# A second pair of weight blocks per layer computed by Strassen's scheme, its weight sums added by VectorE

## The chip, the cores and the metric

The kernel runs on 1 core of one Trainium2 chip. Its metric is the device time of one execution in microseconds (us); before the change the median of 3 runs is 895.15 us (894.86 to 895.54). Five engines with instruction streams of their own work beside each other: PE (TensorE: matmuls; PEld, its weight loads), DVE (VectorE), ACT (ScalarE), POOL (GpSimd) and SP (SyncE, which mostly issues DMA transfers). They wait for each other through semaphores only, and each takes its own instructions in the order in which they are written.

## The reference

A decoder trunk of DEPTH = 2 layers on 256 tokens of width 2048, all in float32. Each layer normalises its input, projects it by one matrix w_in of 2048 x 7,444 into the parts of four groups of attention heads (fox, diff, moba, gla), multiplies each group's output by a gate, and maps the 2048 mixed columns back by w_out, 2048 x 2048:

```python
def hybrid_layer(x, layer_idx, norm_g, w_in, ...):
    h = rms_norm(x, norm_g)
    p = split_columns(jnp.einsum("bsd,de->bse", h, w_in))
    ...
    fox = forgetting_attention(...); fox = from_heads(fox) * jax.nn.silu(p["fox_g"])
    diff = differential_attention(...); diff = from_heads(rms_norm(diff, ...)) * jax.nn.silu(p["diff_g"])
    moba = moba_attention(...); moba = from_heads(moba) * jax.nn.silu(p["moba_g"])
    gla = gla_chunked(...); gla = from_heads(rms_norm(gla, ...)) * jax.nn.silu(p["gla_g"])
    mixed = jnp.concatenate([fox, diff, moba, gla], axis=-1)
    return x + jnp.einsum("bse,ed->bsd", mixed, w_out)
```

## The kernel before

**Three products per multiplication.** TensorE runs in a fast float32 format (fp32r) that keeps fewer bits. So each operand is split into hi, its rounding (`hi_of`, an ACT copy into fp32r), and lo, the residue (`lo_of`, a DVE subtraction), and a product is hi x hi + lo x hi + hi x lo. The normalised input lies transposed in `hTp` (hi and lo), the mixed rows in `mTh` and `mTl`.

**Steps.** The weights stream in from HBM in *steps*, in an order that `_steps` fixes. A plain step is two blocks of 128 rows of one block of up to 512 columns: 512 KB into one of 5 buffers `raw` (issued by SP), a rounding by ACT, a residue by DVE, and 2 x 2 x 3 = 12 matmuls into two PSUM banks (`mm`), one for each half of the tokens. Eight plain steps make a block. hi and lo have 4 buffers each (PART_BUFS), so the splitting runs at most three steps ahead of the multiplying.

**A pair by Strassen's scheme.** Two blocks of 512 columns (`NAMES`) form a 2 x 2 block product: the 256 tokens and the 2048 rows are halved too, and seven products ("forms" p1 to p7) take the place of eight. A form is four steps c0 to c3 of 6 matmuls each, all into one PSUM bank which the pair holds. p1, p2 and p4 multiply plain halves of hTp; p3, p5, p6 and p7 multiply sums of halves, which `sum_forms` computes once per layer and keeps in mTh and mTl. On the weights' side the sums grow in the four chunks of `xs` (called y in the code; the residual rows rest elsewhere meanwhile): y starts as the weights' block 12, then 11, 22 and 21 are added to it while p5, p6, p7 and p4 use it as it then stands. Before, GpSimd adds them by accumulating DMA transfers (`add_to_y`, line 1683). After its last step a form is taken from PSUM into the tile `left` or `right` (`pair_result`, line 1779), scaled by the row's norm: the first of a sum by ACT, the others by DVE with an addition. Matmuls of a later form wait until the bank has been read.

**Order.** The program is written by a planner that keeps a clock for every engine (`Times`, `emit`, `choose`): attention work waits in tasks and is put between the splitting wherever the planner sees an engine free. `MIDDLE` sets the order of the blocks, and `FORMS_AT` the places of the form steps: before, one pair per layer (moba_v and diff_v), at plain steps 3, 6 and 8 of ten blocks, so that a form step stands after every two or three plain ones. The output projection begins with the products of gla and fox, then diff, then moba; the attention results are turned by DVE transposes and two DMA transfers (`turned`) and split into mTh and mTl (`split_group`).

Of the kernel before, what the change touches and what calls it, by code (L numbers as in the profile page):

```python
# [45 lines left out]
BY_DMA = True  # L46
# [3 lines left out]
KEPT = 2  # L50
PATIENCE = 0
HORIZON = 1.5
URGENT_HI = 3.0
URGENT_LO = 2.5
STALL = 0.3
SAFE = 1.0
HANDOVER = 0.2
SOON = 0.5
WAITED = 0.5
EARLY = 4  # L60
LOADED = 6.0
WRITE = 5.0
READ = 7.5
ADDED = 9.5
ISSUE = 0.6
CONSTANT = 12.0
# [90 lines left out]
def _pair_steps(l, n):  # L157
# [3 lines left out]
    if not BY_DMA:  # L161
        raws.update({"p6": ("22",), "p4": ("21",)})
# [4 lines left out]
def _steps():  # L167
# [71 lines left out]
class Times:  # L239


    def __init__(self):
        self.now, self.last, self.ends, self.by, self.free = 0.0, 0.0, {}, {}, {}

# [3 lines left out]
    def of(self, *operands, kind=None):  # L248
        names = [self.name(a) for a in operands if hasattr(a, "shape")]
        return max((self.ends.get(z, 0.0) + HANDOVER * (self.by.get(z) != kind) for z in names), default=0.0)  # L250
# [16 lines left out]
class Timed:  # L267
# [20 lines left out]
    def move(self, out, src, us, **kw):  # L288
        return self.give(Op("d" + self.kind, partial(self.eng.dma_start, out, src, **kw), [src], [out], us))
# [81 lines left out]
def hybrid_trunk(  # L371
# [68 lines left out]
    def emit(op, task=None):  # L440
# [8 lines left out]
        elif op.kind[0] == "d":  # L449
            end = at + op.us  # L450
            if op.kind == "da":
                a_.tail = max(a_.tail, times.now) + ISSUE
        else:
# [5 lines left out]
            e.tail = max(at, e.tail) + us  # L459
            end = e.tail  # L460
# [98 lines left out]
    s4.younger = lambda: len({t.rank for t in tasks if t.rank < cur["task"].rank}) if cur["task"] else 0  # L559
# [113 lines left out]
    def constants():  # L673

        yield from until(("h", 0, 3))
        a_.move(ct, const, 4.5)
        w3 = s2.get([P, DEPTH, 256])
# [24 lines left out]
        a_.move(fb.rearrange("p l h -> p (l h)"), bcast_rows(fox_fb, 0, DEPTH * H), CONSTANT)  # L702
# [9 lines left out]
        for l in range(DEPTH):  # L712
            li = 0.8 - 0.6 * math.exp(-0.3 * l)
            v_.scalar_tensor_tensor(lam[:, l:l + 1], ls2[:, l, 0:1], li, ls2[:, l, 1:2], op0=OP.add, op1=OP.subtract)
            v_.tensor_scalar(dng[:, l:l + 1], dng[:, l:l + 1], 1.0 - li, None, op0=OP.mult)

# [1271 lines left out]
```

## Time and profile before

| | us |
|---|---|
| median of 3 runs | 895.15 (894.86 to 895.54) |
| profiled execution: span from first to last instruction | 891.2 |
| PE, PEld busy | 881.5, 750.8 |
| DVE, ACT, POOL busy | 662.2, 559.1, 60.0 |
| HBM traffic | 254 GB/s over the span |

The profile comes from one execution. Its time outside the span isn't listed; the median stands 3.95 us above its span. Busy times are of one engine each, so they overlap. A matmul's length is modelled and overlaps the next one's, so distances are read from starts.

### The profile page before, as it was taken

Reading aid. Unit: us, or ns where it says so; the run is one execution under the profiler, and the core shown is the slowest. Engines: PE = TensorE matmul, PEld = TensorE weight load, DVE = VectorE, ACT = ScalarE, POOL = GpSimd, SP = SyncE. Lnnn points to the kernel's source line nnn. Section 1 sums busy time; section 2 is a strip of 40 time slices with the busy share of each in tenths; the row PEclk is TensorE's granted clock in tenths of the full one; section 3 lists DMA queues with packets and bytes.
Section 4 is the critical chain, followed back from the end, with each engine's and each line's share of the span. In section 5 each row is a group of like instructions: output and inputs, shape, how many; then the busy total and the mean of one; then the engine's idle time right before and its main releaser. Section 6 shows DMA issues by size and latency. Waiting matters only on the chain.

```text
span 891.2 us, 12456 instructions
## 1 busy us (share of the span) xinstructions
PE 881.5 (99%) x4380; PEld 750.8 (84%) x4380; DVE 662.2 (74%) x943; ACT 559.1 (63%) x846; POOL 60.0 (7%) x87
## 2 busy tenths in 40 slices
PE   9999999999999999999999999999999999999996
PEld 7988889888887888888899888898888888888886
DVE  6689878878867967656679778879676788585583
ACT  7577675577646667644756876578644575693461
POOL 1010110000110000000000100110000100101000
PEclk9999999999999999999999999999999999999999
DMA  8889897747988685977798898878958978499742
GB/s 289 294 263 303 266 301 241 254 147 263 288 240 274 203 317 178 362 265 228 235 302 265 285 320 224 253 227 277 337 147 262 301 220 271 168 301 363 236 143 96
DMA packets 84142, 227.45 MB, mean 255 GB/s; under 512 B 9979, under 2 KB 30443, under 8 KB 83950
## 3 DMA queue, kind: packets, MB, share of 16 engines
q1 hardware_dynamic: 73336, 192.00, 63.9%
q0 software_dynamic: 9152, 33.03, 14.5%
q10 hardware_dynamic: 1590, 1.62, 0.5%
q8 instruction: 34, 0.56, 0.3%
q14 instruction: 30, 0.25, 0.1%
HBM read 204.06 MB, written 22.55 MB: 254 GB/s over the span
## 4 chain that ended last, share of the span: by engine, by line
PE 93%; DVE 2%; DMA 2%; issue 1%; ACT 1%; SPq 0%; POOLq 0%; POOL 0%; DVEq 0%; ACTq 0%
PE mm L466 79%; PE side L466 14%; DMA raw<-in_weights 2%; DVE lo L466 1%; DVE four L466 1%; ACT hi L466 1%; DMA far<-four 0%; DVE mTl L466 0%; ACT four L466 0%; ACT L466 0%; DVE raw L466 0%; DVE eight L466 0%; SPq L466 0%; POOLq L1984 0%; POOL rf L466 0%
## 5 line engine op out<-in xcount | busy, mean ns | idle before, releaser
L466 ACT ACTIVATE hi<-raw 128x1024 fp32r<-128x1024 f32 (+2 forms) x319 | 316.6, 1011 | 190.9 <-PE mm L466 110.2
L466 PE MATMUL mm<-hi,hTp 128*128 128x512 f32 (+1 forms) x1760 | 432.7, 381 | 1.2 <-ACT hTp L466 0.9
L466 DVE TENSOR_TENSOR lo<-raw,hi 128x1024 fp32r<-128x1024 f32 (+2 forms) x319 | 363.7, 1157 | 93.3 <-ACT hi L466 89.0
L466 PEld LDWEIGHTS mm<-hi,hTp 128*128 128x128 f32 x1760 | 321.5, 188 | 60.3 <-ACT hi L466 1.3
L466 PE MATMUL mm<-lo,hTp 128*128 128x512 f32 (+1 forms) x880 | 237.4, 380 | 0.1
L466 PEld LDWEIGHTS mm<-lo,hTp 128*128 128x128 f32 x880 | 162.4, 188 | 30.6 <-DVE lo L466 0.8
L466 PE MATMUL mm<-hi,mTh 128*128 128x512 f32 (+1 forms) x256 | 69.3, 377 | 0.0
L466 PE MATMUL mm<-lo,mTh 128*128 128x512 f32 (+1 forms) x256 | 69.0, 376 | 0.1
L466 PE MATMUL mm<-hi,mTl 128*128 128x512 f32 (+1 forms) x256 | 69.0, 376 | 0.0
L466 PEld LDWEIGHTS mm<-lo,mTh 128*128 128x128 f32 x256 | 46.2, 188 | 9.2 <-DVE lo L466 0.5
L466 PEld LDWEIGHTS mm<-hi,mTl 128*128 128x128 f32 x256 | 46.3, 188 | 8.8
L466 PEld LDWEIGHTS mm<-hi,mTh 128*128 128x128 f32 x256 | 46.0, 188 | 8.6 <-ACT hi L466 0.4
L466 ACT ACTIVATE four<-mm,rstd 128x512 f32<-128x512 f32 (+2 forms) x56 | 36.7, 667 | 26.3 <-PE mm L466 26.3
L466 POOL DMA_DIRECT2D four<-far x40 | 21.8, 546 | 444.0 <-DMA far<-four 193.5
L466 DVE STREAM_TRANSPOSE four<-four 128x1024 f32<-128x1024 f32 (+1 forms) x34 | 39.1, 1149 | 6.7 <-ACT four L466 6.3
L466 ACT ACTIVATE four<-four 128x512 fp32r<-128x512 f32 (+3 forms) x44 | 35.5, 819 | 12.6 <-DMA four<-far 8.8
L466 PEld LDWEIGHTS side<-four,four 128*128 128x128 f32 (+1 forms) x336 | 37.7, 190 | 3.9 <-issue 1.8
L466 PE MATMUL side<-four,four 128*128 128x128 f32 (+3 forms) x336 | 39.3, 281 | 0.0
L1686 POOL DMA_DIRECT2D xs<-in_weights x24 | 21.2, 900 | 169.5 <-DVE lo L466 36.2
L466 DVE TENSOR_TENSOR lo<-xs,hi 128x1024 fp32r<-128x1024 f32 x24 | 29.1, 1214 | 1.8 <-ACT hi L466 1.8
L466 ACT ACTIVATE mTh<-four 128x1024 fp32r<-128x1024 f32 x16 | 16.9, 1057 | 21.2 <-DVE four L466 21.1
L466 ACT ACTIVATE hi<-xs 128x1024 fp32r<-128x1024 f32 x24 | 25.4, 1060 | 7.1 <-PE mm L466 6.2
(146 smaller groups left out, 685.1 us busy)
## 6 DMA issues: line engine op xcount, KB each, us to landing
raw<-in_weights SPq DMA_DIRECT2D x271, 512.0 KB, 4.9
four<-far POOLq DMA_DIRECT2D x34, 512.0 KB, 6.7
far<-four SPq DMA_DIRECT2D x128, 128.0 KB, 3.9
raw<-in_weights SPq DMA_DIRECT2D x46, 348.0 KB, 5.1
xs<-in_weights POOLq DMA_DIRECT2D x24, 512.0 KB, 8.5
xs<-in_weights SPq DMA_DIRECT2D x8, 512.0 KB, 8.3
xs<-in_x SPq DMA_DIRECT2D x4, 512.0 KB
kept<-xs SPq DMA_DIRECT2D x1, 2048.0 KB, 10.6
```

Source lines behind the costliest of these rows:

```text
L466: op.do()
L1686: g_.eng.dma_start(ys[:, c], weights[at:at + P * 1024].rearrange("(p j c) -> p j c", p=P, j=2), accum_op=OP.add)
```

## The change

The pair diff_q and diff_k is computed by forms too, ahead of moba_v and diff_v, in both layers. The forms come in the order 1 5 3 6 7 2 4. The weights' sums are added by VectorE (`add_raw`): block 11, 22 and 21 arrive as `raw` for the forms p1, p3 and p2 anyway, and are added to y from there, after which the raw buffer is free; the accumulating transfers are gone. `pair_result` takes p1 out twice by ACT and everything else by DVE. The form steps stand where a table of 56 places per layer puts them, counted in plain steps of the layer, most of them closer together than before. The order of the blocks, the places where the residual rows come back (`X_AT`), and the planner's prices and rules change too. In layer 1 `sum_forms` reads the unsplit tiles of the input, which are kept until then, where it added hi and lo before.

```diff
-X_AT = (1, 5, 9, 13)
-MIDDLE = ("gla_v", "fox_q", "fox_k", "fox_v", "fox_g", "diff_q", "diff_k", "moba_q", "moba_k", "diff_g", "moba_g", "moba_v", "diff_v")
-NAMES = (("moba_v", "diff_v"),)
+X_AT = (5, 8, 11, 13)
+MIDDLE = ('gla_v', 'fox_k', 'fox_q', 'fox_v', 'fox_g', 'moba_q', 'diff_k', 'moba_k', 'moba_g', 'moba_v', 'diff_q', 'diff_g', 'diff_v')
+NAMES = (('diff_q', 'diff_k'), ('moba_v', 'diff_v'))
...
-FORMS_AT = {3: (3, 6, 8), 4: (3, 6, 8), 5: (3, 6, 8), 6: (3, 6, 8), 7: (3, 6, 8), 8: (3, 6, 8), 9: (3, 6, 8), 10: (3, 6, 8), 11: (3, 6, 8), 12: (3,)}
-FORM_ORDER = ("p2", "p5", "p3", "p1", "p6", "p7", "p4")
+FORMS_AT = ((33, 34, 34, 35, 36, 39, 39, 39, 41, 42, 43, 43, 43, 45, 47, 47,
...
+FORM_ORDER = ("p1", "p5", "p3", "p6", "p7", "p2", "p4")
+ADDED_BY_V = ("p1", "p3", "p2")
+LATE = FORM_ORDER[0] == "p1"
+STARTS = ("p1", "p5", "p6", "p2", "p4") if LATE else ("p1", "p5", "p2")
...
     for l in range(DEPTH):
         rest = deque(z for n in range(len(NAMES)) for z in _pair_steps(l, n))
-        for i, places in FORMS_AT.items():
-            own = [k for k, s in enumerate(steps) if s.get("block") == l * LAYER + i]
-            for z, at in enumerate(places):
-                steps.insert(own[0] + at + z, rest.popleft())
+        own = min(k for k, s in enumerate(steps) if s.get("block", -1) // LAYER == l)
+        for z, at in enumerate(FORMS_AT[l]):
+            steps.insert(own + at + z, rest.popleft())
...
+    def add_raw(s):
+        y = ys[:, s["c"]]
+        v_.tensor_add(y, y, s["raws"][0])
+        yield
+        y_at[s["c"]] = s["slots"][0][0] = times.of(y)
...
+        whole = [env["t", l, c] for c in range(4)] if l else None
...
+            if whole:
+                if len(terms) == 3:
+                    sums(v_.tensor_sub, terms[0], terms[2])
+                else:
+                    sums(v_.tensor_add if terms[0] > 0 else v_.tensor_sub, None, terms[1])
...
+        if f in ADDED_BY_V:
             y_at[c] = math.inf
-            added.append((end, partial(add_to_y, s, q)))
+            begin(add_raw(s), -1, 3)
...
+        if LATE:
+            if f == "p1":
+                evac(left[:, 0], 0)
+                evac(left[:, 1], 1)
+            elif f == "p5":
+                add(right[:, 1], 1, left[:, 1], OP.subtract)
+            elif f == "p3":
+                add(right[:, 0], 0, left[:, 0], OP.subtract)
+            elif f == "p6":
+                add(right[:, 0], 0, by=nr)
+            elif f == "p7":
+                add(right[:, 1], 1, by=nr)
+                add(left[:, 1], 1)
+                given(l, s["id"][1], 1, right)
+            elif f == "p2":
+                add(left[:, 0], 0)
+            else:
+                add(left[:, 1], 1)
+                given(l, s["id"][1], 0, left)
```

(`evac` is an ACT copy out of PSUM, `add` a DVE scalar_tensor_tensor on it.)

How instructions move is shown at three places. Numbers behind names tell one tile of a name from the next; "waits" names the engines whose semaphores a row waits for.

TensorE in layer 0, before, at the change from form p5 to form p3: the second of the two plain steps between them (hi_1291, lo_1292), then p3's first step in the pair's bank mm2 (hi_1311, lo_1312):

```order
L466 MATMUL mm1_1149<-hi_1291,hTp_112 128x512 [waits Activation_49]
L466 MATMUL mm1_1149<-hi_1291,hTp_112 128x512 x3
L466 MATMUL mm1_1149<-lo_1292,hTp_112 128x512 [waits DVE_49]
L466 MATMUL mm1_1149<-lo_1292,hTp_112 128x512
L466 MATMUL mm3_1150<-hi_1291,hTp_112 128x512 x4
L466 MATMUL mm3_1150<-lo_1292,hTp_112 128x512 x2
L466 MATMUL mm2_758<-hi_1311,mTh_113 128x512 [waits Activation_49]
L466 MATMUL mm2_758<-hi_1311,mTh_113 128x512
L466 MATMUL mm2_758<-hi_1311,mTl_114 128x512 x2
L466 MATMUL mm2_758<-lo_1312,mTh_113 128x512 [waits DVE_49]
L466 MATMUL mm2_758<-lo_1312,mTh_113 128x512
```

TensorE in layer 0 of the first pair, after, from form p3's last step (mm0, hi_1285 and lo_1286) to p6's first (hi_1295 and lo_1296):

```order
L478 MATMUL mm0_923<-hi_1285,mTh_113 128x512 [waits Activation_49]
L478 MATMUL mm0_923<-hi_1285,mTh_113 128x512
L478 MATMUL mm0_923<-hi_1285,mTl_114 128x512 x2
L478 MATMUL mm0_923<-lo_1286,mTh_113 128x512 [waits DVE_49]
L478 MATMUL mm0_923<-lo_1286,mTh_113 128x512
L478 MATMUL mm0_923<-hi_1295,mTh_113 128x512 [waits DVE_49,Activation_49]
L478 MATMUL mm0_923<-hi_1295,mTh_113 128x512
L478 MATMUL mm0_923<-hi_1295,mTl_114 128x512 x2
L478 MATMUL mm0_923<-lo_1296,mTh_113 128x512 x2
L478 MATMUL mm1_1213<-hi_1337,hTp_112 128x512 [waits Activation_49]
```

No plain step stands between these two forms, and p6's first matmul into mm0 waits for DVE, which has to take p3 out of mm0; before, p3's first matmul waited for nothing but its rounding by ACT.

VectorE in layer 0, before, at the same change from p5 to p3 (lo_1312 is p3's first residue; tq and eight belong to gla's attention):

```order
L466 TENSOR_TENSOR lo_1292<-raw_1171,hi_1291 128x1024 [waits DVE_49,DMAHW7_49,PE_49,Activation_49]
L466 TENSOR_TENSOR tq_97<-eight0_1184,four2_1096 64x2x64 x2
L466 TENSOR_TENSOR lo_1312<-raw_1245,hi_1311 128x1024 [waits DMAHW0_49,PE_49,Activation_49]
L466 TENSOR_TENSOR tq_97<-eight0_1184,four2_1096 64x2x64 x2
L466 TENSOR_TENSOR lo_1337<-raw_1268,hi_1336 128x696 [waits DMAHW1_49,PE_49,Activation_49]
L466 TENSOR_TENSOR tq_97<-eight0_1184,four2_1096 64x2x64 x3
L466 TENSOR_TENSOR eight0_1184<-eight0_1184,four2_1096 128x2x64
L466 TENSOR_TENSOR lo_1351<-raw_1281,hi_1350 128x696 [waits DMAHW2_49,PE_49,Activation_49]
```

VectorE in layer 0, after, at the change from p3 to p6 of the first pair (the rows xs<-xs,raw add weights, the last row takes p3 out of PSUM):

```order
L478 TENSOR_TENSOR lo_1262<-raw_1197,hi_1261 128x1024 [waits DMAHW1_49,PE_49,Activation_49]
L478 TENSOR_TENSOR xs_83<-xs_83,raw_1197 128x1024
L478 TENSOR_TENSOR qx_94<-eight0_911,four13_807 64x128 x2
L478 TENSOR_TENSOR lo_1286<-raw_1221,hi_1285 128x1024 [waits DMAHW2_49,PE_49,Activation_49]
L478 TENSOR_TENSOR xs_83<-xs_83,raw_1221 128x1024
L478 TENSOR_TENSOR lo_1296<-xs_83,hi_1295 128x1024 [waits PE_49,Activation_49]
L478 COPY_PREDICATED four2_910<-masks_84,side1_1301 128x8x16 [waits PE_49,Activation_49]
L478 COPY_PREDICATED four2_910<-masks_84,side1_1301 128x16x8 [waits DVE_49]
L478 COPY_PREDICATED four2_910<-masks_84,side1_1301 128x32x4 [waits DVE_49]
L478 TENSOR_TENSOR lo_1338<-raw_1248,hi_1337 128x1024 [waits DMAHW7_49]
L478 SCALAR_TENSOR_TENSOR four4_1189<-mm0_923,rstd_585,four0_1019 128x512 [waits PE_49]
```

Where one residue per step stood with attention's small operations between, a form step now has a residue and an addition, and the evacuation stands behind the residue of the step after next.

GpSimd, before, from the row norms of layer 0 on (xs<-in_weights are the accumulating transfers, four<-far are returns of turned rows):

```order
L466 TENSOR_TENSOR rstd<-pw,halfpow 128x2
L1686 DMA xs<-in_weights 128x1024 x5
L466 DMA four_1019<-far_1039 128x1024
L1686 DMA xs<-in_weights 128x1024 x2
L466 DMA four_1141<-far_1128 128x1024
L466 DMA four_1142<-far_1147 128x1024
L1686 DMA xs<-in_weights 128x1024
```

GpSimd, after, from the same place:

```order
L478 TENSOR_TENSOR rstd<-pw,halfpow 128x2
L478 DMA four_680<-far_723 128x1024
L478 DMA four_1101<-far_1099 128x1024
L478 DMA four_1226<-far_1228 128x1024
L478 DMA four_1553<-far_1605 128x1024
L478 DMA four_1831<-far_1841 128x1024
```

The 24 accumulating transfers are gone from GpSimd's queue; the returns of turned rows follow each other.

More of the change, by code (lines that the diff above doesn't have):

```diff
@@ L49 @@
 T4 = 14
-KEPT = 2
+KEPT = 1
 PATIENCE = 0
 HORIZON = 1.5
-URGENT_HI = 3.0
+URGENT_HI = 3.5
 URGENT_LO = 2.5
 STALL = 0.3
-SAFE = 1.0
+DELAY = 0.2
+LEAD = 3.0
+OVERLAP = 0.085
+SAFE = 1.5
 HANDOVER = 0.2
-SOON = 0.5
-WAITED = 0.5
-EARLY = 4
+SOON = 1.0
+WAITED = 0.8
+EARLY = 5
 LOADED = 6.0
-WRITE = 5.0
-READ = 7.5
-ADDED = 9.5
+WRITE = 4.0
+READ = 11
+ADDED = 12.5
 ISSUE = 0.6
+RATE = 340000.0
+LANDING = 3.2
 CONSTANT = 12.0
@@ L449, in emit @@
         elif op.kind[0] == "d":
-            end = at + op.us
+            end = times.land(at, op.moved, op.us)
             if op.kind == "da":
@@ L1182, in fox_forget @@
         yield
+        yield from until("loaded")
         v_.tensor_add(fx, fx, fb[:, l, None, :].to_broadcast([P, 2, H]))
@@ L1284, in diff @@
         yield from until(("diff_k", l))
+        yield from until("lam")
         yield
@@ L1526, in load_more @@
             s = plan[i]
-            if kind == "raw" and loads["out"] == RAW_BUFS and not (loads["freed"] and loads["freed"][0] <= by):
-                return
+            if len(loads["ring"]) == RAW_BUFS:
+                freed = loads["ring"][0][0]
+                if freed is None or freed > by:
+                    return
+                loads["ring"].popleft()
+            s.setdefault("slots", []).append([None])
+            loads["ring"].append(s["slots"][-1])
             if "pair" in s:
@@ L1532, in load_more @@
                 load(i)
-            if kind == "raw" and loads["out"] == RAW_BUFS:
-                loads["freed"].popleft()
-            else:
-                loads["out"] += kind == "raw"
             loads["next"] += 1
@@ L1635, in sum_forms, with sums @@
         z = yield from s4.take([P, 8, P])
+        whole = [env["t", l, c] for c in range(4)] if l else None
+        def sums(op, a, b):
+            for i in range(2):
+                o = z[:, i * 4:i * 4 + 4]
+                first, second = (o if not q else whole[(int(q[1]) - 1) * 2 + i][:, :, (int(q[0]) - 1) * P:int(q[0]) * P] for q in (a, b))
+                op(o, first, second)
         def part(x, k, m):
@@ L1659, in sum_forms @@
         s4.put(z)
+        if whole:
+            s4.put(*whole)
         given_out(("forms", l))
@@ L1775, in multiply_form @@
         for i, (x, part, j) in enumerate(products):
-            matmul(o, lhs(x, j), s[part][:, j], main=True, start=f in ("p1", "p5", "p2") and s["first"] and i == 0, stop=s["last"] and i == 5,
-                   skip_group_check=f in ("p3", "p6", "p7", "p4"))
+            matmul(o, lhs(x, j), s[part][:, j], main=True, start=f in STARTS and s["first"] and i == 0, stop=s["last"] and i == 5, skip_group_check=f not in STARTS)
     def pair_result(s):
@@ L1890, in hybrid_trunk @@
     x_at = {outer[l] + k: (l, c) for l in range(DEPTH) for c, k in enumerate(X_AT)}
+    assert all(max(i for i, s in enumerate(plan) if s.get("pair") == l) < outer[l] + X_AT[0] for l in range(DEPTH))
     load_more()
@@ L1912, in hybrid_trunk @@
         if banks["s"] is not None and "done" in pairs[banks["s"]]:
-            banks["next"].append(pairs[banks["s"]]["bank"])
+            banks["next"].insert(1, pairs[banks["s"]]["bank"])
             banks["s"] = None
```

83 lines of the change are left out of this document (51 added, 32 removed).

## The prediction

> **What bounds the kernel now.** I read the page's busy line first, then the chain of waits, then what TensorE waited for, then the timeline of its matmuls.
>
> ```profile
> span 891.2 us, 12456 instructions
> PE 881.5 (99%) x4380; PEld 750.8 (84%) x4380; DVE 662.2 (74%) x943; ACT 559.1 (63%) x846; POOL 60.0 (7%) x87
> PEclk9999999999999999999999999999999999999999
> PE 93%; DVE 2%; DMA 2%; issue 1%; ACT 1%; SPq 0%; POOLq 0%; POOL 0%; DVEq 0%; ACTq 0%
> ```
>
> The first two lines show TensorE busy all through, at full granted clock, with VectorE at 74%. The chain that ended last lies 93% on PE. A busy TensorE need not be a full one, so the next view is needed:
>
> ```profile
> PE mm L466 <- ACT hTp L466: 0.9, 1, 0.9
> PE side L668 <- PEq L1977: 0.8, 1, 0.8
> PE mm L466 <- DVE hTp L466: 0.2, 1, 0.2
> ```
>
> These are all the waits put down to PE, 1.9 us, and the first two belong to the start. The timeline shows that what lies between is issued back to back (start, length, instructions; lengths overlap, so I use starts):
>
> ```profile
> 506.98 1.98 PE L466 MATMUL mm<-hi,hTp 128*128 128x512 f32 x8
> 508.80 1.07 PE L466 MATMUL mm<-lo,hTp 128*128 128x512 f32 x4
> 509.70 1.98 PE L466 MATMUL mm<-hi,hTp 128*128 128x512 f32 x8
> 494.92 0.80 PE L466 MATMUL side<-hi,hTp 128*128 128x348 f32 x4
> 495.55 0.48 PE L466 MATMUL side<-lo,hTp 128*128 128x348 f32 x2
> ```
>
> From 506.98 to 509.70 stand twelve 512-column matmuls: 0.227 us each. So a plain step (two row blocks of weights, 12 matmuls) is 2.72 us and a form step (6 matmuls) 1.36 us; four 348-column matmuls take 0.63 us, so a 348-column step takes 1.90. A matmul removed is 0.227 us off the path, if the operands of the others still arrive.
>
> **The change, part by part: TensorE.** A pair of blocks costs 2 x 8 plain steps, 192 matmuls, when done plainly, and 7 x 4 form steps, 168 matmuls, as forms. The second pair saves 24 per layer, 48 in all (1504+752 on hTp fall by 240, three groups of 64 on mTh and mTl come): 48 x 0.227 = **-10.9 us**. The start and the end of the program keep their steps, so this comes off the path whole unless stalls give it back.
>
> **What pays for it: VectorE.** Groups by form (busy us, mean ns):
>
> ```profile
> L466 DVE TENSOR_TENSOR lo<-xs,hi 128x1024 fp32r<-128x1024 f32 x24 | 29.1, 1214 | 1.8 <-ACT hi L466 1.8
> L466 DVE TENSOR_TENSOR raw<-xs,raw 128x1024 f32<-128x1024 f32 x8 | 9.8, 1220 | 0.3 <-DMA raw<-in_weights 0.3
> L466 DVE SCALAR_TENSOR_TENSOR four<-mm,rstd,four 128x512 f32<-128x512 f32 x2 | 1.5, 751 | 3.1 <-PE mm L466 3.1
> L466 DVE TENSOR_TENSOR four<-four,hTp 128x1024 f32<-128x1024 f32 x16 | 19.5, 1221 | 0.2
> L466 ACT ACTIVATE hi<-xs 128x1024 fp32r<-128x1024 f32 x24 | 25.4, 1060 | 7.1 <-PE mm L466 6.2 <-ACT four L466 0.7
> L466 ACT ACTIVATE four<-mm,rstd 128x512 f32<-128x512 f32 x48 | 32.4, 688 | 22.8 <-PE mm L466 22.7
> ```
>
> VectorE gets 48 additions of weights and 8 differences (raw<-xs,raw is the nearest row, 1.22), 24 residues (1.21), 22 evacuations of a form (0.75), and eight more operations of 512 columns (5 us); layer 1's sums from whole tiles save 10 operations of 1.22. Together 56 x 1.22 + 24 x 1.21 + 22 x 0.75 + 5 - 12 = **+107 us**: 662 becomes about 769, 87% of a span of 880. ScalarE gets 24 roundings (25.4 us) and loses 8 evacuations (5.5): 63% becomes 66%, beside TensorE throughout, cost 0. GpSimd loses 24 accumulating transfers, SP gets 8 loads:
>
> ```profile
> raw<-in_weights SPq DMA_DIRECT2D x271, 512.0 KB, 4.9
> xs<-in_weights POOLq DMA_DIRECT2D x24, 512.0 KB, 8.5
> ```
>
> With the 8 loads more that is 16 transfers of 512 KB fewer, and additions that took 8.5 us to land become 1.2 us on VectorE. A gain here shortens nothing, since TensorE did not wait for them. Against it stands that a raw buffer added by VectorE is held until the addition (5 buffers, 4.9 us to refill); that cost is VectorE's lateness again and is counted there.
>
> The average of 87% decides nothing; the form steps lie in one run per layer. What VectorE needs when it never waits is read from starts in this stretch:
>
> ```profile
> 153.94 0.89 DVE L466 TENSOR_TENSOR eight<-four 128x128 f32<-128x128 f32 x4
> 154.75 0.88 DVE L466 TENSOR_TENSOR lo<-raw,hi 128x696 fp32r<-128x696 f32 x1
> 155.54 0.49 DVE L466 TENSOR_TENSOR eight<-four 128x128 f32<-128x128 f32 x2
> 155.94 1.22 DVE L466 TENSOR_TENSOR lo<-raw,hi 128x1024 fp32r<-128x1024 f32 x1
> 157.08 0.90 DVE L466 TENSOR_TENSOR eight<-four 128x128 f32<-128x128 f32 x4
> 157.88 1.23 DVE L466 TENSOR_TENSOR lo<-raw,hi 128x1024 fp32r<-128x1024 f32 x1
> ```
>
> A 1024-wide operation takes 1.14 (155.94 to 157.08), a 696-wide one 0.79, a 128-wide one 0.20 (four from 157.08 to 157.88): each 0.085 less than its length. A form step has one residue and, in 16 of 28 steps, an addition or difference more: 1.8 us of VectorE a step against 1.36 of TensorE. By the new order of VectorE, summed with these prices, the run of layer 0 (first form step to the last but two) needs 246 us of VectorE in 251 us of TensorE, 98%; layer 1's 260 in 279, 93%; before, the same run of layer 0 needed 194 in 239, 81%.
>
> The worst stretch goes from the third p1 step of layer 0 to the third p7 step of its first pair. VectorE has 45 operations of 1024 (51.3), 83 of 128 (16.6), 3 of 696 (2.4), 3 evacuations (0.751 less 0.085, 2.0) and 7 others (1.8), with the first residue (1.14) 75.2 us. TensorE has 16 form steps (21.8), 14 plain (38.1), 3 of 348 columns (5.7) and 16 attention matmuls, for which the chain has a row (start, length, what):
>
> ```profile
> 143.25 1.56 PE side L466 x14
> 525.03 0.04 issue
> 525.07 18.43 PE mm L466 x80
> ```
>
> 1.56 / 14 = 0.11 each, 1.8: 67.4 us. With 4 buffers of parts VectorE can begin at most three steps ahead (5.4 us), and the last residue is needed 0.9 into its step: 73.7. At full use VectorE is 1.5 us late. Can it be used fully?
>
> ```profile
> 550.00:575.00 25.00, 25.00 (x112) 20.71 (x111) 24.52 (x57) 14.56 (x17) 3.16 (x4) 1.00 0.94 248
> 725.00:750.00 25.00, 25.00 (x112) 20.71 (x111) 24.35 (x41) 16.45 (x30) 1.13 (x2) 1.00 0.76 231
> ```
>
> Here it was busy 24.5 and 24.4 of 25 us, 98%, while TensorE stood still for nothing. At 98% the stretch takes 76.7 us: **+3.0**. The other dense stretches stay 1 to 2 us inside their lead by the same sum: 0.
>
> **The forms' one bank.** Evacuations now follow every form but the first on VectorE, and the next form's first matmul waits for them. Before, two or three plain steps lay between forms; now it is one at twelve changes of form, and none at p3 to p6 of layer 0. That last one costs 0.67 of VectorE plus the handover (0.04 by the chain's row above); it lies inside the worst stretch and is in its sum. With one step of 2.72 between, an evacuation of 0.67 (two after p7) behind one residue of 1.14 needs at most 2.5: covered. Where the step is a 348-column one (after the first p7 of layer 1) 1.90 is 0.6 short: **+0.6**. One more residue ahead in the queue would make 12 changes cost 5.5 together: bounds 0 and 5.5. Queued behind a waiting evacuation on VectorE are the next steps' residues, so TensorE would wait for these too.
>
> **The end of the layer.** The pair with moba_v and diff_v ends inside the output projection, so diff's last chain has less room. Its length now:
>
> ```profile
> 344.02 1.25 DVE L466 STREAM_TRANSPOSE four<-four 128x1024 f32<-128x1024 f32 x1
> 359.08 1.14 ACT L466 ACTIVATE four<-four,dng 128x1024 f32<-128x1024 f32 x1
> 361.35 1.23 DVE L466 TENSOR_TENSOR mTl<-four,mTh 128x1024 fp32r<-128x1024 f32 x1 [0.91 <-ACT mTh L466]
> ```
>
> From the transpose (through two transfers) to the residue's end: 18.6 us. In the new order the product ahead of that transpose stands behind p4's evacuation, which TensorE releases 26 us (layer 0) and 24 us (layer 1) before it needs the result; 0.7 for the evacuation, 1.1 for the product and these 18.6 leave 4 to 6 us. Cost 0; bounds 0 and some 3 per layer if the transfers are slow.
>
> **Sum** against the profiled execution: 891.2 - 10.9 + 3.0 + 0.6 = 883.9 of span; the median, 895.15, is 3.95 above this span, and I take that as fixed: **887.9, called 888.0**.
>
> **Rivals.** (1) *VectorE is used 92 to 95%, not 98%.* The worst stretch at 95% is 79.2, +5.5 (890.4); at 92% the whole run of layer 0 takes 267.5 against 251 and 6 of lead, +10.3 (894.6). For it: on average VectorE idled 26%. Against: it idles when it is ahead, and the two windows show 98% where it was needed. (2) *Slower:* it is used under 92%, because residues wait for roundings, and evacuations for TensorE, in order. At 90% layer 0 loses 16.2 and layer 1 4.1: 904.6. It decides at 91.8%, where layer 0 loses 10.9. It would also come about if each operation cost its full length: 364 and 382 operations x 0.085 add 31 and 32, so the runs lose 20 and 8: 912. The starts above speak against that. A rule of the Trainium skill speaks for it: "VectorE: DVE Perf Modes", section "The DRAIN you can't avoid", lets the next operation start only when the pipe is empty, and adds that one which is not held starts earlier. By its first half the price is the 1.22 of the records, by its second less; the 1.14 between starts agrees with the second. (3) *A late chain at the outputs* by slow transfers, 2 to 4 us late a layer beyond its room: 892 to 896. For it: the room is only 4 to 6 us. Against: the 18.6 us hold two transfers in a kernel that moves more. (4) *The count does not fall:* excluded, since the new order has the 48 matmuls fewer.
>
> **How the numbers follow.** The forecast (VectorE 95.5% or better, 884 to 890) gets 0.64; rival 1 above 93% (890 to 893.3) 0.14; rivals 1 and 3 at about no change 0.10; slower 0.10, of it 0.03 for full lengths; still faster than 884, with no stall and the few small stalls of now gone, 0.02. What a measurement can tell from no change is 0.2%, 893.4 to 896.9. So faster 0.80, same 0.10, slower 0.10. The range goes from 883.5 (all costs at their lower end) to 896.0, which takes in both bounds for the changes of form and rival 1 down to 92%.
>
> **What will show it.** TensorE with 48 matmuls fewer and as good as no waits outside layer 0's first run; there, matmuls waiting for VectorE's residues, 3 us in all; VectorE at 98% in those windows, some 770 us busy in total; at p3 to p6 one gap near 1 us. Wrong: waits of TensorE on VectorE in layer 1, waits on mTl at the outputs, or VectorE idle inside layer 0's run.

## The result, and the profile after

The changed kernel takes 889.0 us (median of 4 runs, 888.74 to 889.38) against 895.0 us before (4 runs beside it, 892.92 to 895.54): a ratio of 0.9939, 95% interval 0.9925 to 0.9953. It is 6.0 us faster; 888.0 had been forecast. The page of the profile after, its head and the lines that answer to those of before (busy us, share of the span, instructions; then the chain):

```profile
span 886.9 us, 12492 instructions
PE 873.2 (98%) x4332; PEld 742.8 (84%) x4332; DVE 753.9 (85%) x1043; ACT 580.9 (66%) x864; POOL 39.2 (4%) x63
PE 85%; DVE 10%; issue 2%; DMA 1%; ACT 1%; SPq 0%; POOLq 0%; DVEq 0%; POOL 0%; ACTq 0%
```

TensorE has 48 matmuls fewer (4332 for 4380) and 8.3 us less busy time, VectorE 92 us more. The span fell by 4.3 us, not by the 10.9 that 48 matmuls are worth, and VectorE now holds 10% of the chain that ended last, where it held 2%. What TensorE waited for (us in total, times, longest):

```profile
PE mm L478 <- DVE lo L478: 3.0, 1, 3.0
PE mm L478 <- DVE four L478: 0.9, 1, 0.9
PE mm L478 <- ACT four L478: 0.6, 1, 0.6
```

One wait is for a residue, one for a bank that VectorE takes out, and one is small. Three more, two of them at the start, last 1.3 us together. Where they lie is read from the busy time by stretch (PE, PEld, DVE, ACT, POOL with instructions; then granted clock, DMA share, GB/s):

```profile
75.00:100.00 25.00, 25.00 (x114) 20.68 (x113) 25.00 (x30) 19.68 (x28) 0.00 (x0) 1.00 0.78 272
100.00:125.00 25.00, 21.95 (x89) 17.48 (x88) 24.78 (x56) 16.19 (x18) 0.54 (x1) 0.93 0.48 152
125.00:150.00 25.00, 24.07 (x122) 20.21 (x122) 24.67 (x48) 13.90 (x21) 0.53 (x1) 1.00 0.65 213
150.00:175.00 25.00, 24.67 (x133) 21.74 (x133) 23.55 (x41) 11.52 (x15) 0.53 (x1) 1.00 0.65 199
600.00:625.00 25.00, 24.29 (x140) 21.94 (x139) 23.23 (x36) 17.46 (x21) 0.00 (x0) 1.00 0.74 247
```

From 100 to 175 us TensorE is idle for 3.05 + 0.93 + 0.33 us. From 100 to 125 us its granted clock is 0.93 on average, which is another 1.75: 6.1 us. This is a half clock: from 106.51 us on the clock is 0.50 for 3.41 us. With the 0.71 at 600 to 625 us that is 6.8, and -10.9 + 6.8 = -4.1 against the measured -4.3. VectorE is full from 75 us on: 98.0 of 100 us. Around the long wait (start, length, engine, what, and in brackets idle time and its end):

```profile
98.00 1.22 DVE L478 TENSOR_TENSOR lo<-raw,hi 128x1024 fp32r<-128x1024 f32 x1
...
100.86 1.50 DVE L478 TENSOR_TENSOR eight<-four 128x128 f32<-128x128 f32 x7
...
103.67 1.70 DVE L478 TENSOR_TENSOR eight<-four 128x128 f32<-128x128 f32 x8
105.28 1.22 DVE L478 TENSOR_TENSOR lo<-raw,hi 128x1024 fp32r<-128x1024 f32 x1
...
106.56 1.65 PE L478 MATMUL mm<-lo,hTp 128*128 128x512 f32 x3 [3.05 <-DVE lo L478]
```

Between two residues (98.00 and 105.28) VectorE does 6 us of other work without a pause: gla's additions (the rows eight<-four), the tail of the sums of activations, a few small constants. The residue at 98.00 was ready 1.4 us ahead of its matmul, which started at 100.63; TensorE uses that up and runs dry. This is layer 0, first pair, the second plain step behind the first p5 step.

### The profile page after: what moved, and what is told of

The parts are those of the page before. It is cut to its first block, busy times and chain, and to the rows that moved or that the text cites. A ratio compares the mean times of both kernels' runs of the same rounds, so it can differ in the third digit from the quotient of the medians.

```text
span 886.9 us, 12492 instructions
## 1 busy us (share of the span) xinstructions
PE 873.2 (98%) x4332; PEld 742.8 (84%) x4332; DVE 753.9 (85%) x1043; ACT 580.9 (66%) x864; POOL 39.2 (4%) x63
## 3 DMA queue, kind: packets, MB, share of 16 engines
q10 hardware_dynamic: 1590, 1.62, 0.6%
## 4 chain that ended last, share of the span: by engine, by line
PE 85%; DVE 10%; issue 2%; DMA 1%; ACT 1%; SPq 0%; POOLq 0%; DVEq 0%; POOL 0%; ACTq 0%
PE mm L478 72%; PE side L478 14%; DVE lo L478 4%; DVE four L478 2%; DMA raw<-in_weights 1%; DVE eight L478 1%; DVE xs L478 1%; DVE raw L478 1%; DMA far<-four 0%; ACT hi L478 0%; DVE mTl L478 0%; DVE tq L478 0%; DVE at L478 0%; ACT four L478 0%; SPq L478 0%
## 5 line engine op out<-in xcount | busy, mean ns | idle before, releaser
L478 PE MATMUL mm<-hi,hTp 128*128 128x512 f32 (+1 forms) x1600 | 393.8, 380 | 1.0 <-ACT four L478 0.6
L478 PEld LDWEIGHTS mm<-hi,hTp 128*128 128x128 f32 x1600 | 292.4, 188 | 54.7 <-ACT four L478 0.9
L478 PE MATMUL mm<-lo,hTp 128*128 128x512 f32 (+1 forms) x800 | 217.6, 380 | 3.1 <-DVE lo L478 3.0
L478 PE MATMUL mm<-hi,mTh 128*128 128x512 f32 (+1 forms) x320 | 89.5, 381 | 1.2 <-DVE four L478 0.9
L478 PE MATMUL mm<-hi,mTl 128*128 128x512 f32 (+1 forms) x320 | 89.0, 379 | 0.0
L478 PE MATMUL mm<-lo,mTh 128*128 128x512 f32 (+1 forms) x320 | 88.9, 379 | 0.1
L478 DVE TENSOR_TENSOR lo<-xs,hi 128x1024 fp32r<-128x1024 f32 x48 | 58.1, 1216 | 4.6 <-ACT hi L478 4.6
L478 ACT ACTIVATE hi<-xs 128x1024 fp32r<-128x1024 f32 x48 | 50.4, 1056 | 14.5 <-PE mm L478 13.8
L478 DVE TENSOR_TENSOR xs<-xs,raw 128x1024 f32<-128x1024 f32 x48 | 58.3, 1215 | 0.0
L478 DVE TENSOR_TENSOR four<-four,four 128x512 fp32r<-128x512 f32 (+4 forms) x37 | 30.8, 846 | 3.7 <-ACT four L478 3.5
```

The lines of the kernel that those rows point to most:

```text
L478: op.do()
```

## The experiments

Two questions were open: is the loss between 100 and 175 us a matter of the *amount* of VectorE's work there (theory A: it is full, so whatever stands first the sum stays), or of its *order* (theory B: one residue stands behind work that could wait)? And what is the half clock behind the wait? Times are medians; ratios are to the kernel before, timed beside each run. The changed kernel stands at 889.0 us and 0.9939.

| run | us | ratio, 95% interval |
|---|---|---|
| need | 913.99 | 1.0206 (1.0186 to 1.0226) |
| p6_later | 890.46 | 0.9948 (0.9934 to 0.9963) |
| hold3, hold6 (one execution each) | 894.53, 897.97 | |
| add_gp_l0 | 905.65 | 1.0119 (1.0104 to 1.0134) |
| add_gp | 947.42 | 1.0588 (1.0571 to 1.0606) |
| add_dma | 928.0 | 1.0367 (1.0352 to 1.0383) |
| one_pair | 967.6 | 1.0808 (1.079 to 1.0826) |
| less4 | 886.8 | 0.9918 (0.9897 to 0.994) |
| less8 | 887.56 | 0.9918 (0.9901 to 0.9935) |
| dma8 | 892.62 | 0.998 (0.997 to 0.9989) |
| sooner | 891.85 | 0.9964 (0.995 to 0.9978) |

**need.** A form step waits in the planner for its own sum only, and a block that needs a second bank pair waits for it there.

```diff
- ... {("forms", l)} if z["form"] in SUM_OF ...
+ ... {("forms", l, SUM_OF[z["form"]])} if z["form"] in SUM_OF ...
...
             lo_of(mTf[1][:, f], z, mTf[0][:, f])
+            given_out(("forms", l, f))
...
-        given_out(("forms", l))
...
+                    while not side.free:
+                        tick(False)
                     b["side"] = side.get([P, 1024])
```

> Edit: in the planner a p5, p3, p6 or p7 step waits for its own sum of activations, no longer for all four sums. Nothing is computed otherwise; the planner's clock no longer stands still for 6 us at the first p5 step, so residues that it had put behind the additions of gla (eight<-four, 15 x 0.2 us) should come ahead of them. Theory A (the 3.05 us wait at 103 us is VectorE's capacity: it is full from 75 to 135 us): the wait moves to another residue before 150 us, TensorE loses the same 4 to 6 us there, and the whole is within 1 us of 889.0. Theory B (the wait is a matter of order): no wait over 0.5 us and full granted clock from 75 to 125 us, 889.0 - 3.05 - 1.6 = 884.4. Either way the order of the later work changes with the planner's clock, which may cost something at the end of layer 0.

The wait at 103 us went, and another came 25 us later, again with a half clock. The timeline of that place:

```profile
129.31 1.21 DVE L478 TENSOR_TENSOR xs<-xs,raw 128x1024 f32<-128x1024 f32 x1
130.44 1.21 DVE L478 TENSOR_TENSOR lo<-raw,hi 128x1024 fp32r<-128x1024 f32 x1
131.58 0.73 DVE L478 SCALAR_TENSOR_TENSOR four<-mm,rstd,four 128x512 f32<-128x512 f32 x1
...
132.46 1.19 PE L478 MATMUL mm<-hi,mTh 128*128 128x512 f32 x2 [3.42 <-DVE four L478]
```

The bank's evacuation stands behind an addition and a residue on a full VectorE. So the loss in this run moved, as theory A has it, from a residue to an evacuation. Most of the 25 us by which the run is slower than the changed kernel lie at the end of layer 0, whose work the planner's changed clock shifts: from 375 to 425 us TensorE loses 16.6 us, 11.3 of them in waits for the outputs (`PE side <- ACT four`, 8.4 us in two waits, and `PE mm <- ACT mTh`, 2.9 in one), the rest at half clock.

**p6_later.** One plain step is put between p3 and p6 of layer 0's first pair (the table's 13th place, 43, becomes 44; the 14th stays at 45).

> Edit: in layer 0 the first p6 step of the first pair stands one plain step later, so that one plain step lies between p3's last step and p6's first. Theory (the wait at 136 us is the handover of the one bank: evacuation 0.67 us behind p3's last matmul): the 0.93 us wait for four<-mm is gone, 888.0. Rival (VectorE is short there anyway): the wait comes back as one for a residue within the next 15 us, 889.0.

The rival held in kind. The wait at 136 us is gone (125 to 150 us: PE 25.00), and in its place stands a wait for a residue, 18 us later and not within 15, behind eleven tq; the time is 1.5 us above the rival's 889.0:

```profile
150.59 3.29 DVE L478 TENSOR_TENSOR tq<-eight,four 64x128 f32<-64x128 f32 x11
153.80 1.21 DVE L478 TENSOR_TENSOR lo<-raw,hi 128x1024 fp32r<-128x1024 f32 x1
155.07 0.74 PE L478 MATMUL mm<-lo,hTp 128*128 128x512 f32 x2 [0.84 <-DVE lo L478]
```

**hold3, hold6.** At one place where VectorE is half idle (it came at 424 us, not near 388), three or six copies into the bank that the next matmul needs:

```diff
                     b["banks"], b["ps"] = zip(*[take_bank() for _ in range(2)])
+                if i == HELD:
+                    for _ in range(3):
+                        v_.eng.tensor_copy(b["ps"][0], plan[i - 1]["block"]["ps"][1])
```

> Edit: before the first matmul of the last output block but one of layer 0 (near 388 us, VectorE half idle) VectorE copies a finished 128x512 bank three times into the bank that this matmul overwrites, so TensorE stands still for about 3 x 0.67 = 2.0 us. If a stall costs its length: +2 us against after, clock 1.00. If every stall over 1 us is followed by half clock: +3.6 or more and the granted clock below 1.00 in that stretch.

> Edit: the same with six copies, about 4 us of standing still. If the half clock after 103 us in the changed kernel was the stall's doing: matmuls at 0.427 us start to start behind it for about 3 us, so +4.0 + 1.6 = 5.6 us against after, and a granted clock below 1.00 in that stretch. If the low clock at 106 us had another cause: +4.0 and full clock.

With the residual's two additions ahead of the copies, the waits were 3.55 and 5.75 us. Matmul by matmul against the changed kernel, TensorE falls 5.5 and 7.4 us behind at this place: the wait and some 1.7 us of half clock. The +5.5 and +9.0 us of the whole are of one execution each; hold6 has small waits elsewhere too. Behind the first wait (hold3):

```profile
427.20 0.70 PE L479 MATMUL mm<-hi,mTh 128*128 128x512 f32 x2 [3.55 <-DVE mm L2024]
427.74 0.63 PE L479 MATMUL mm<-hi,mTl 128*128 128x512 f32 x2
...
428.73 1.06 PE L479 MATMUL mm<-hi,mTh 128*128 128x512 f32 x2
```

A pair first takes 0.63, then 1.06: the array goes on at full rate for 1.5 us and only then falls to half (the pair after the last shown starts at 429.58, 0.85 later: 0.43 for each matmul). In hold6 the low rate begins with the first pair. So the half clock is the wait's doing. But it is not a matter of this one wait's length: in hold6 the wait at 103 us of the changed kernel is there too, 3.03 us long, and no half clock follows. TensorE's timeline in hold6, then the last of these matmuls in the changed kernel:

```profile
107.28 1.20 PE L479 MATMUL mm<-lo,hTp 128*128 128x512 f32 x4 [3.03 <-DVE lo L479]
...
114.63 0.73 PE L479 MATMUL mm<-lo,mTh 128*128 128x512 f32 x2 [1.16 <-DVE lo L479]
...
122.38 0.62 PE L479 MATMUL mm<-hi,mTh 128*128 128x512 f32 x2
```

```profile
121.66 0.61 PE L478 MATMUL mm<-hi,mTh 128*128 128x512 f32 x2
```

Without the half clock TensorE catches up with VectorE and waits 1.16 us for the second p5 residue. Behind the first wait hold6 stands 0.72 us behind the changed kernel (107.28 and 106.56), and 15 us later still 0.72 (122.38 and 121.66). In the changed kernel the half clock therefore cost nothing on balance: TensorE would have waited for VectorE instead. That is evidence for theory A. Why half clock follows one wait and not the other stands in the last section.

**add_gp_l0, add_gp.** The additions of weights go to GpSimd: for layer 0's first pair (`g_ if s["id"] == (0, 0) else v_`), or all 48. For the first pair these are twelve additions, four of them for p2 late in the pair, where the expectation counts eight; the wait for a bank that it names is not in this edit.

```diff
-        v_.tensor_add(y, y, s["raws"][0])
+        (g_).tensor_add(y, y, s["raws"][0])
```

> Edit: the eight additions of weights (xs<-xs,raw) of layer 0's first pair are done by GpSimd in place of VectorE; a block that needs a second bank pair waits for it in the planner. Theory A (layer 0's first run is bound by VectorE's capacity: from the third p1 residue to the third p7 residue it needs 78 us in 72): seven of the eight additions lie in that stretch and take 7 x 1.14 = 8.0 us off VectorE, so the waits of 7 us in all between 100 and 170 us fall to under 1 us: 889.0 - 6.5 = 882.5. Theory B (the order decides, not the amount): a wait of 3 us or more for a residue stays in that stretch, 886 or more. Rival C: an addition on GpSimd is so slow (128x8 takes 2.0 us there) or slows VectorE's operations so much that the next form's weights or residues come late: 890 or more, and the mean of lo<-raw,hi 128x1024 rises above 1.22 us.

> Edit: all 48 additions of weights by GpSimd. Theory A: VectorE falls from 754 to about 696 us, no wait of TensorE for a residue in any run of forms; what is left are the start, the changes of form (0.6 in layer 1) and the end: 882. Theory B: as the changed kernel, waits of some us in layer 0, 886 or more. Rival C: GpSimd too slow or VectorE slowed: 890 or more.

Rival C won, by far more than its price. Groups by operation between 75 and 150 us in add_gp (busy, mean ns):

```profile
L478 DVE TENSOR_TENSOR lo<-raw,hi 128x1024 fp32r<-128x1024 f32 x22 | 30.9, 1410 | 0.1
L478 DVE TENSOR_TENSOR tq<-eight,four 64x128 f32<-64x128 f32 x14 | 8.1, 580 | 0.2
```

These took 1217 and 285 ns in the same stretch of the changed kernel. GpSimd's own addition had a mean of 3161 ns (48 of them, 151 us). VectorE was busy for 72.9 of these 75 us although the additions had left it, against 74.5 in the changed kernel. The runs say nothing of A against B. The Trainium skill, "GPSIMD Engine Reference", section "2. Architecture", says that GpSimd's one read and one write port to the buffers are shared with VectorE; the longer means above agree with that.

**add_dma.** `ADDED_BY_V = ()`: the additions are accumulating transfers again.

> Edit: all 48 additions of weights by accumulating transfers, as the kernel before does them; order and second pair as changed. Theory A: VectorE gets the same relief as with GpSimd, so no wait for residues in layer 0's first run; if the transfers (8.5 us each before) land within the 14 us between a p1 step and the p5 step of the same rows: 882. Rival: they land late, and TensorE waits for a rounding that waits for xs<-in_weights: 890 or more.

The rival held. Waits of TensorE over the whole run:

```profile
PE mm L478 <- ACT hi L478: 15.5, 12, 5.2
PE mm L478 <- ACT mTh L478: 12.6, 1, 12.6
...
PE mm L478 <- DVE lo L478: 1.6, 3, 0.9
```

Residues are hardly waited for now, but roundings are (of weights that land late: 9.8 us from issue to landing, where it was 8.5 before), and the outputs. In the stretch from 100 to 175 us itself TensorE loses 2.4 us, at full clock, against 6.1, and 0.94 of them are again a wait for the bank: there the relief of VectorE works, as theory A has it. Planned with transfers, the closer order loses more elsewhere than that.

**one_pair.** `NAMES = (("moba_v", "diff_v"),)`, with the second half of each layer's table (its places moved by the 16 plain steps that come in ahead of it) and the wait for a bank as in need.

> Edit: only the pair with moba_v and diff_v is done by forms, in the changed order, with additions by VectorE and at the places that its forms have now; diff_q and diff_k are done plainly. 24 matmuls more a layer: +48 x 0.227 = 10.9 us on TensorE. If the 7 us that TensorE loses in the changed kernel come from the first pair's dense run in layer 0, they go: 889.0 + 10.9 - 6.5 = 893.4. If they come from the order of forms or from the additions as such: 898 to 900.

The time is a miss of another kind: TensorE waits for the outputs (`PE mm <- ACT mTh`, 40.2 us in two waits, and `PE side <- ACT four`, 21.0 in three). The likely reason is that diff_q, now done plainly, comes eleventh of the thirteen middle blocks, and diff's chain is late with it; that was not tried. Only the stretch in question can be used, and there TensorE loses nothing:

```profile
100.00:125.00 25.00, 25.00 (x128) 21.29 (x128) 22.73 (x59) 12.65 (x21) 1.07 (x2) 1.00 0.64 210
```

Gla's additions and its tq stand in this part of the run too. So VectorE's other work alone does not make the loss; as far as this run, planned anew, can tell, it takes the first pair's form steps beside it.

**less4, less8.** VectorE's additions for p1 (less4), and for p1 and p3 (less8), of layer 0's first pair are not issued; the planner's clock counts them still, so that all else keeps its place. The two kernels thus leave out a part of the weights' sums and do not compute the reference; they serve for their times alone. This takes the order's changes out of the question. The edit of less8:

```diff
-        v_.tensor_add(y, y, s["raws"][0])
+        us = v_.fixed + v_.per * 1024
+        if s["id"] == (0, 0) and s["form"] in ("p1", "p3"):
+            give(Op("v", lambda: None, [y, s["raws"][0]], [y], us))
+        else:
+            v_.tensor_add(y, y, s["raws"][0])
```

> Leaves out the four additions of weights of p1 in layer 0's first pair (VectorE, at 83 to 94 us in the changed kernel); every other instruction stands in its old order on its engine, and p5, p3, p6 and p7 multiply by other numbers. TensorE loses 7.3 us between 100 and 175 us in the changed kernel, the half clock after 106 us among it. Theory A (amount of VectorE work): 4 x 1.14 = 4.6 us less work, so 2.7 us are left of the loss and the time is 889.0 - 4.6 = 884.4; the wait of 3.05 us at 103 us is gone and the half clock with it. Theory B (order: what stands ahead of that one residue): it comes 4.6 us earlier too, so the wait at 103 us goes as well, but the waits after 110 us stay at 2.2 us and the half clock's 1.6 goes besides: 889.0 - 5.1 = 883.9. What tells them apart is the stretch from 110 to 130 us: under A residues there have almost no lead again or a new wait, under B leads of 3 us or more.

> Leaves out the eight additions of weights of p1 and p3 in layer 0's first pair, all else in its old order. Theory A: 9.1 us less VectorE work against a loss of 7.3: no wait over 0.5 us and full clock from 75 to 175 us, 889.0 - 7 = 882. Theory B (a wait that has its place in the order, like the bank's handover at 136 us): 0.93 us stay there, 883.

Both took longer than either theory had it (886.8 against 884.4 and 883.9, 887.6 against 882 and 883), and they came out alike. The stretch from 100 to 125 us of less4, then this and the next of less8:

```profile
100.00:125.00 25.00, 23.57 (x102) 18.49 (x101) 24.48 (x50) 16.23 (x19) 0.54 (x1) 1.00 0.52 157
```

```profile
100.00:125.00 25.00, 23.57 (x101) 18.50 (x100) 24.42 (x53) 16.23 (x19) 1.07 (x2) 1.00 0.56 175
125.00:150.00 25.00, 24.07 (x122) 20.20 (x121) 20.19 (x47) 13.47 (x22) 0.00 (x0) 1.00 0.48 169
```

Without the first four additions 1.62 of the 3.05 us idle go and the whole half clock, 3.4 of 6.1 us by these stretches. From one matmul to another it is 2.8 us: from the residue matmul at 100.63 to p6's first at 137.27 the changed kernel takes 36.6 us, less4 33.9 (100.77 to 134.62) and less8 33.8 (100.66 to 134.50). The next four are worth nothing. They stand behind the waits of the first stretch and could help only in the second, where VectorE now idles for 4.8 us and the wait of 0.93 us for the bank stays: that wait is order. The 1.4 us left in the first stretch stand where VectorE is still busy for 24.4 of 25 us; that order makes them is read from VectorE's timeline in less8:

```profile
94.09 1.22 DVE L478 TENSOR_TENSOR lo<-raw,hi 128x1024 fp32r<-128x1024 f32 x1
...
102.51 1.22 DVE L478 TENSOR_TENSOR lo<-raw,hi 128x1024 fp32r<-128x1024 f32 x1
...
106.24 3.58 DVE L478 TENSOR_TENSOR tq<-eight,four 64x128 f32<-64x128 f32 x12
```

Here the residue at 94.09 is ready over five us before its matmul (100.66), about as early as four buffers of parts let it be; still the next one starts 8.4 us after it, and the full lead is gone (TensorE waits 0.24 us). The twelve tq then cost a wait of 1.13 us.

**dma8.** The same eight additions as accumulating transfers, put into the program where VectorE had them, while the planner still counts them for VectorE.

```diff
-        v_.tensor_add(y, y, s["raws"][0])
...
+            give(Op("v", partial(g_.eng.dma_start, y, src, accum_op=OP.add), [y, s["raws"][0]], [y], us))
```

> The eight additions of p1 and p3 in layer 0's first pair are done by accumulating transfers on GpSimd's queue at the same places in the program; all else is computed as in the changed kernel and stands in its order, and the result is the reference's. Theory A: VectorE gets the same 9.1 us as without them, and if the transfers land in time (8.5 to 10 us against 13 us from the first p1 step to the first p5 step) 882 to 883. Rival: xs<-in_weights lands after the rounding of p5 or p6 wants it, or slows the raw loads: waits of TensorE on roundings (hi) in layer 0's first run, 886 or more.

The rival held: the time is 3.6 us above the changed kernel's. From 75 to 100 us TensorE waits 3.3 us for roundings of raw blocks that land late, at a DMA share of 1.04 (0.78 in the changed kernel); the eight transfers took 12.3 us to land (median).

```profile
75.00:100.00 25.00, 21.65 (x94) 16.66 (x94) 17.00 (x22) 16.65 (x24) 0.85 (x1) 1.00 1.04 316
```

**sooner.** Theory B's remedy on the changed kernel itself: the two residues that stood behind gla's additions come right behind their roundings. In the planner's `run_stage`, for these two steps:

```diff
         do()
+        if i in SOONER and kind == "a":
...
+            lo_of(s["lo"], s["raws"][0] if s.get("from") else s["raw"] if "raw" in s else ys[:, s["c"]], s["hi"])
```

(The stage that stood later keeps its price in the planner and issues nothing.)

> Only two residues move: those of the two plain steps after the first p5 step (fox_k's third and second last but one) go from behind the additions of gla, lam and one mTl to right behind their roundings, 9 to 17 VectorE instructions earlier; the planner's clock and every other instruction's order stay, and the amount of VectorE's work too. Theory A (VectorE is full here, so whatever goes ahead of it the sum stays): with the changed kernel's durations the wait at 103 us is gone, the next residue (first of the p5 steps after it) comes 1.2 us late and the one behind twelve tq<-eight,four of 0.30 us another 3.3 us, 4.5 in all against 3.05 and 1.6 of half clock before: 889 within 1 us. Theory B (the order of this one place costs 3 to 5 us that are VectorE's to give): no wait over 1 us between 100 and 120 us, 884 to 886.

TensorE's timeline:

```profile
109.07 0.73 PE L479 MATMUL mm<-lo,mTh 128*128 128x512 f32 x2 [1.16 <-DVE lo L479]
110.70 0.73 PE L479 MATMUL mm<-hi,mTh 128*128 128x512 f32 x2 [0.90 <-ACT hi L479]
...
114.43 1.22 PE L479 MATMUL mm<-lo,mTh 128*128 128x512 f32 x2 [2.33 <-DVE lo L479]
```

The wait at 103 us is gone, and 1.16 + 0.90 + 2.33 = 4.4 us come in its place, where theory A had 1.2 and 3.3. The clock is low again, for 6.83 us from 111.53 on, ahead of the longest of these waits, where it was 3.41 in the changed kernel. The whole is slower than the changed kernel by 2 to 3 us, more than A allowed. Matmul by matmul in the profiled execution, TensorE is 2.1 us further behind by 121 us; another 1.9 come after 600 us, in small waits. Theory B's 884 to 886 is out.

**What follows.** At this place both theories hold in part. While VectorE is full, moving work only moves the wait (need, p6_later, sooner). Taking the first four additions away gives 2.8 us, and then no more (less4 against less8): about half of the loss is amount. The 0.93 us for the bank are order, and for the remaining 1.4 us between 100 and 125 us order is read from the timeline and not tried apart from the amount. None of the runs that compute the reference beats the changed kernel. Whether an order exists that places gla's blocks between the residues in smaller pieces and keeps the end of layer 0 as it is was not found out.

## Why the prediction came out as it did

**TensorE, -10.9: right.** 48 matmuls went, and -10.9 with the losses read from the stretches above makes the span's change.

**VectorE, +107 us: right as a sum of lengths.** Summed over the groups by form, the lengths rose by 104 us. The busy time rose by 92 only, 754 where some 770 were expected: two operations whose lengths overlap count once in it, and more of them now follow back to back.

**VectorE's use, 98%: right.** In the worst stretch, from the third p1 residue (its start, 87.58) to the end of the third p7 residue (166.54), it was busy for 78.16 of 78.96 us, 99%:

```profile
87.58:166.54 78.96, 74.70 (x345) 61.62 (x343) 78.16 (x144) 46.03 (x61) 1.07 (x2) 0.98 0.57 187
```

Rival 1 (92 to 95%) gave a loss of the size that came, but by a cause that wasn't there.

**The worst stretch, +3.0: the step that failed.** Its sum was 75.2 of work against 73.7 of time. Three numbers in it were off. First, *the work*: the 83 operations of 128 were all priced at 0.20. In the changed kernel 28 of them are tq, of 64 partitions:

```profile
L478 DVE TENSOR_TENSOR tq<-eight,four 64x128 f32<-64x128 f32 x28 | 8.0, 286 | 0.4
```

They show the same length as the others, but no overlap: twelve took 3.58 us in less8, 0.30 each, and the trace of before had a row that says so (seven at 127.41 in 2.10). That is 28 x 0.10 = 2.8 us. Ten more of the 83 are copies under a mask, 0.35 us long; by their starts they took 0.33 each, 1.3 us more in all:

```profile
L478 DVE COPY_PREDICATED four<-masks,side 128x128 f32<-128x128 uint8 x10 | 3.5, 352 | 0.2
```

The seven others took some 0.8 less than their 1.8. So the sum would have been 78.5, near the 79.0 us that the stretch took. Second, *the lead*: "VectorE can begin at most three steps ahead (5.4 us)" is the bound of the buffers and was taken as the fact. VectorE was full from 75 us on, with the sums of activations and gla, and came to the stretch with no such lead: its first residue began at 87.58, 1.7 us ahead of its step's first matmul (89.26 below). Third, *the matmuls*: 32 of attention lie in the stretch, not 16, 1.8 us more for TensorE, which gives VectorE time. So 79.0 us, against 1.7 + 69.2 + 0.9 = 71.8: 7.2 late, where the prediction had 1.5 at full use and 3.0 at 98%. The work adds 3.8 to the 1.5, the lead 3.7, and the matmuls take off 1.8. TensorE's first matmuls of the two steps:

```profile
89.26 1.07 PE L478 MATMUL mm<-hi,hTp 128*128 128x512 f32 x4
...
165.31 0.73 PE L478 MATMUL mm<-hi,mTh 128*128 128x512 f32 x2 [0.24 <-ACT hi L478]
```

They stand 76.05 us apart with 69.2 us of matmuls between: 6.85 lost (the stretches above count 6.1 of it as idle or half clock). The sum should have begun where VectorE became full, not where the forms begin. And it took the order as free: without the eight additions, 9.1 us of VectorE, it would have given no loss, and in less8 2.7 us were there.

**p3 to p6 without a step between, near 1 us: right** (0.93), and its cause as well, since less8 keeps it with VectorE idle around it. But p6_later shows that while VectorE is full it is no cost of its own.

**Layer 1's first p7 to p2, +0.6: right.** The second evacuation of p7 and the first matmul of p2:

```profile
605.55 0.74 DVE L478 SCALAR_TENSOR_TENSOR four<-mm,rstd,four 128x512 f32<-128x512 f32 x1
...
606.44 1.17 PE L478 MATMUL mm<-hi,hTp 128*128 128x512 f32 x4 [0.62 <-ACT four L478]
```

The profile names ACT, but the matmul starts 0.15 us after the evacuation's end.

**The outputs, 0: right for this kernel,** with no wait on mTh or mTl. The runs show how narrow that is: need, add_dma and one_pair, each planned anew with a change early in a layer, had single waits of 5.1, 12.6 and 20.4 us at the outputs.

**GpSimd's transfers, no gain: right against the kernel before, incomplete for the order chosen.** With all additions by transfers the run planned otherwise alike takes 928.0, so the gain was had only with them off that queue.

**The total was nearer than its terms.** The span was forecast 3.0 us too short (883.9 for 886.9). The second error is the 3.95 us around the span that the prediction took as fixed. In every run of the record a run's time stands 1.7 to 2.0 us above its own span, 1.84 for the profiled execution after (888.74 and 886.9). So the profiled execution before, with its span of 891.2, was one of about 893.0 us (an estimate; the result lists 892.92 as the lowest of its four), 2.1 below the median of 895.15 that it stood for. Of the 3.95 only some 1.8 go with every run; the other 2.1 were the luck of one execution and did not carry over, and what the slower executions before lost is on no profile. The spans of the two profiled executions differ by 4.3 us, the medians by 6.0. The error of 3.0 in the span and that of 1.85 around it (3.95 against 889.0 - 886.9 = 2.1) had opposite signs: that 888.0 came out so near 889.0 is luck in part. The half clock was not in the prediction at all; by hold6 it cost nothing on balance.

## What to carry to other kernels

Where an engine that feeds the bottleneck gets more work, sum its work from the place where it *becomes* full, with the lead that it then has, not from the place of the change with the lead that the buffers allow. Look also for blocks of its other work between two pieces that the bottleneck waits for: a block longer than the lead costs time even where the engine idles afterwards. And price an operation by starts in a row of its own shape; one length in the records can hide two prices (0.20 and 0.30 us).

## What the runs showed of the hardware

*The half clock follows the idle time in fixed windows of 3.41 us, and not the length of one wait.* In these traces the granted clock is 1.00 or 0.50, and ahead of the program's end each low stretch lasts 3.41 us or a whole multiple of it (6.83 in sooner, 10.24 in add_dma). Counted in steps of 3.41 us back from where the clock changes, the windows tell the cases apart. Two of the changed kernel, three of hold6, two of sooner (columns as above: first the length and the time that TensorE was busy in it, and the granted clock behind POOL):

```profile
103.10:106.51 3.41, 0.41 (x2) 0.00 (x0) 3.41 (x15) 2.31 (x5) 0.00 (x0) 1.00 0.01 2
106.51:109.92 3.41, 3.36 (x8) 2.72 (x9) 3.37 (x7) 2.88 (x4) 0.00 (x0) 0.50 0.58 174
```

```profile
102.45:105.86 3.41, 1.80 (x8) 1.14 (x7) 3.41 (x17) 2.55 (x4) 0.00 (x0) 1.00 0.11 41
105.86:109.28 3.42, 2.00 (x9) 1.66 (x10) 3.42 (x6) 3.15 (x5) 0.00 (x0) 1.00 0.29 92
109.28:112.69 3.41, 3.41 (x17) 2.83 (x16) 3.29 (x11) 2.45 (x3) 0.54 (x1) 1.00 0.71 214
```

```profile
108.12:111.53 3.41, 1.56 (x6) 0.97 (x6) 2.81 (x8) 3.41 (x6) 0.54 (x1) 1.00 0.57 171
111.53:114.95 3.42, 1.09 (x3) 0.50 (x2) 3.32 (x9) 2.45 (x4) 0.00 (x0) 0.50 0.40 138
```

The changed kernel's wait of 3.05 us lies in one window, 3.00 us of it idle, and the next window is at half clock. The wait of 3.03 us in hold6 falls across two windows, 1.61 and 1.42 us, and the clock stays. In sooner 1.85 us of idle time in one window were enough, from two waits of 1.16 and 0.90 us. In hold3 the wait of 3.55 us splits into 1.51 and 2.04 us, so the fall comes at the end of the second window, 1.5 us after the matmuls had resumed; in dma8 2.23 of a wait of 2.42 us lay in one. Over all traces here, from full clock, every window with 2.0 us idle or more was followed by half clock and none with 1.81 or less; of those between, five were and two were not. At half clock the matmuls take 0.43 us each. The Trainium skill, "TensorE: Matmul & The Clock Gate", section "Part 1: The HAM clock gate (the "warmup" mystery)", has the clock fall after one idle window of about 3.4 us that runs freely. The traces agree with the length and with windows that do not follow the kernel's waits; but here a window need not be idle throughout, some 1.9 of its 3.41 us were enough.

*GpSimd beside VectorE.* An addition of 128x1024 took 3.2 us on GpSimd on average over add_gp, and from 75 to 150 us VectorE's 64-partition multiplications took 0.58 us there on average, for 0.29 in the changed kernel.

*VectorE's operations of 64 partitions* (tq) start 0.30 us apart at a length of 0.29, those of 128 partitions (eight<-four) 0.20 apart at about the same length. Whether the partitions or something else between them makes the difference was not tried.
